# RMSNorm with swish: all transfers issued from SyncE's queue in one written order, with a ring of 100 rows

## The chip, the core and the metric

The kernel runs on one core of a Trainium2 chip. The metric is the time of one execution in device microseconds, as the median of several runs. Beside it stands one execution taken by the hardware profiler, whose span runs from the first to the last instruction of the program. Of the core's engines four are used: VectorE (DVE), ScalarE (ACT), GpSimd (POOL) and SyncE (SP). TensorE does nothing here. Transfers between DRAM and the on-chip memory run on 16 DMA engines, which the queues of SyncE (q1 in the profile) and ScalarE (q10) share.

## The reference

The input x has 16 x 1024 rows of 512 floats. Each row is divided by its root mean square, multiplied by gamma and put through swish:

```python
rms = np.sqrt(np.mean(x ** 2, axis=-1, keepdims=True) + eps)
x_norm = x / rms * gamma
return (x_norm * (1.0 / (1.0 + np.exp(-x_norm)))).astype(np.float32)
```

The 16384 rows of 2 KB are 33.55 MB in and as much out.

## The kernel before, in words

The 16384 rows lie as 128 partitions times 128 rows, so "a row" below means one row of each partition: 128 x 512 floats, 256 KB. The rows are cut into groups of 16, 16, 32, 32, 16 and 16; inside a group each partition holds neighbouring rows of DRAM, so that a piece of n rows is one run of n x 2 KB for each partition.

All rows live in one buffer, `xb`, a ring of 96 rows (line 29); row a sits at place a modulo 96, is loaded there, normalised and swished in place, and stored from there. Rows 96 to 127 reuse places 0 to 31, so they can be loaded only when the first stores have landed.

Compute goes by chunks of four rows (`cn`), 32 chunks, k = 0 to 31, each through four steps:

- `square(k)` on ScalarE: two rows with a sum accumulated along the way (line 181, into `junk`), two rows squared into PSUM (line 188, `sq`). Before it ScalarE waits for the load that holds the chunk (line 178).
- `sums(k)` on VectorE reduces `sq` (line 234), and GpSimd adds eps and takes the power -1/2 (lines 162 and 169).
- `norm(k)` on VectorE multiplies each of the four rows by its factor and gamma (line 245).
- `swish(k)` on ScalarE, one instruction on four rows (line 200).

ScalarE's program is written out as square(k), then swish(k - 2); VectorE's as sums(k), then norm(k - 1). Each engine runs its instructions in the order written.

Transfers are lists of pieces (first row, number of rows). SyncE issues the ten loads (line 125): seven at the start, one after the other, then rows 96 to 127 in three pieces, each after waiting for the stores that empty its places (line 123; `behind` lets load (96,16) also wait for store (16,12)). ScalarE issues the eight stores (line 210) between its own computing: a store stands in ScalarE's program two chunks after its rows are done, and `hold` moves the first three stores to chunk 12, behind a wait for load (64,28) (line 208), and the fourth and later ones to chunk 22 or after, behind a wait for load (112,12). SyncE waits for the remaining stores at the end (line 267).

Two small transfers, a blank one to scratch (line 214) and gamma (line 218), go out on ScalarE's queue at the start. The change leaves them, the compute steps and their order as they are.

Of the kernel before, what the change touches and what calls it, by code (L numbers as in the profile page):

```python
# [9 lines left out]
def kernel(  # L10
# [7 lines left out]
    nc = tc.nc  # L18
# [5 lines left out]
    xf = x.flatten_outer_dims()  # L24
    of = out.flatten_outer_dims()
    R, D = xf.shape

    groups = [16, 16, 32, 32, 16, 16]
    ring = 96
    loads = [(0, 4), (4, 4), (8, 8), (16, 16), (32, 32), (64, 28)]  # L30
    loads += [(92, 4), (96, 16), (112, 12), (124, 4)]
    stores = [(0, 16), (16, 12), (28, 4), (32, 32), (64, 32)]
    stores += [(96, 16), (112, 8), (120, 8)]
    hold = {0: ((64, 28), 12), 3: ((112, 12), 22)}
    behind = {(96, 16): (16, 12)}
    early = 2
    cn = 4
    n_sq = 2
# [9 lines left out]
        assert sum(n for _, n in pieces) == rows_each  # L48

    K = rows_each // cn  # L50
    hold = {t: (loads.index(piece), k) for t, (piece, k) in hold.items()}
    behind = {loads.index(a): stores.index(b) for a, b in behind.items()}
    landings, seen = [], 0
    for k in range(K):
        landings.append([])
# [4 lines left out]
    ends = [-(-(a + n) // cn) for a, n in stores]  # L60
# [20 lines left out]
    ld = [nc.alloc_semaphore(f"ld{t}") for t in range(len(loads))]  # L81
    st = [nc.alloc_semaphore(f"st{t}") for t in range(len(stores))]
# [14 lines left out]
    s_swish = nc.alloc_semaphore("s_swish")  # L97

    def need(ins, sem, value):
        return ins.wait_op(sem, value, "sem-ge")  # L100

    def dram(ap, piece):
        a, n = piece
        g = max(g for g in range(len(groups)) if first[g] <= a)
        r = a - first[g]
        assert r + n <= groups[g], piece
        rows = ap[P * first[g] : P * (first[g] + groups[g])]
        return rows.rearrange("(p n) d -> p n d", n=groups[g])[:, r : r + n, :]

    def buf(piece):  # L110
        a, n = piece
        at = a % ring
        assert at + n <= ring, piece
        return xb[:, at : at + n, :]

    stored_by_sync = set()

    def load(i):
        a, n = loads[i]
        for u, (c, m) in enumerate(stores):  # L120
            over = c + ring < a + n and a < c + m + ring
            if (over or behind.get(i) == u) and u not in stored_by_sync:
                nc.sync.wait_ge(st[u], 16)
                stored_by_sync.add(u)
        return nc.sync.dma_start(  # L125
            out=buf(loads[i]), in_=dram(xf, loads[i])
        ).then_inc(ld[i], 16)

    entry = nc.main_func.blocks[0].instructions
    here = nc.cur_bb.bb.instructions  # L130
# [11 lines left out]
    for t in range(early):  # L142
        ins = load(t).ins
        assert here[-1] is ins or here[-1].name == ins.name
        here.pop()
        at = next(
            i for i, other in enumerate(entry)
            if other.engine == mybir.EngineType.SP
            and isinstance(other, mybir.InstDrain)
        )  # L150
        entry.insert(at, ins)
    for t in range(early, len(loads)):
        load(t)
    nc.sync.wait_ge(s_scratch, 16)

    nc.gpsimd.memset(blank, 0.0).then_inc(s_blank, 1)  # L156
# [3 lines left out]
    for k in range(K):  # L160
        need(
            nc.gpsimd.tensor_scalar(  # L162
                out=aeps[:, k, :], in0=ms[:, k, :], scalar1=eps_f, scalar2=None,
# [6 lines left out]
                out=rstd[:, k, :], in0=aeps[:, k, :], in1=neg_half, op=ALU.pow  # L170
# [4 lines left out]
    def square(k):  # L175
        at = k * cn % ring
        for landing in landings[k]:
            nc.scalar.wait_ge(ld[landing], 16)  # L178
        for j in range(n_sq, cn):
            n = k * (cn - n_sq) + j - n_sq  # L180
            acc = nc.scalar.activation(  # L181
                out=junk[n % 2], in_=xb[:, at + j, :], func=AF.Square,
                scale=inv_d**0.5, accum_out=ms[:, k, j : j + 1],
            )
            if n >= 2:
                need(acc, s_acc, n - 1)
            acc.then_inc(s_acc, 1)
        square = nc.scalar.activation(  # L188
            out=sq[k % 2], in_=xb[:, at : at + n_sq, :],
            func=AF.Square, scale=inv_d**0.5,  # L190
        )
        if k >= 2:
            need(square, s_sum, k - 1)
        square.then_inc(s_sq, 1)

    def swish(k):
        at = k * cn % ring
        rows = xb[:, at : at + cn, :]
        need(
            nc.scalar.activation(out=rows, in_=rows, func=AF.Silu), s_norm, k + 1  # L200
        ).then_inc(s_swish, 1)

    def after(t):
        return max((k for u, (_, k) in hold.items() if u <= t), default=0)

    def store(t):
        if t in hold:
            nc.scalar.wait_ge(ld[hold[t][0]], 16)
        need(
            nc.scalar.dma_start(out=dram(of, stores[t]), in_=buf(stores[t])),  # L210
            s_swish, ends[t],
        ).then_inc(st[t], 16)

    need(nc.scalar.dma_start(out=scratch, in_=blank), s_blank, 1).then_inc(
        s_scratch, 16
    )
# [2 lines left out]
        s_zero, 1,  # L219
    ).then_inc(s_gld, 16)  # L220
    nc.scalar.preload_act_table_set("silu_and_others")  # L221
    stored = 0
    for k in range(K + 3):
        if k < K:
            square(k)
        while stored < len(stores) and max(ends[stored] + 2, after(stored)) <= k:
            store(stored)
            stored += 1
        if 2 <= k < K + 2:
            swish(k - 2)  # L230

    def sums(k):
# [29 lines left out]
        if k >= 1:  # L262
            norm(k - 1)

    for t in range(len(stores)):
        if t not in stored_by_sync:
            nc.sync.wait_ge(st[t], 16)


# [33 lines left out]
```

## Time and profile before

| | before |
|---|---|
| time, median of 3 runs (lowest to highest) | 160.34 us (160.22 to 160.51) |
| span of the profiled execution | 159.3 us (159.28) |
| what lies around the span, median less span | 1.06 us |
| ScalarE busy | 129.7 us, 81% |
| VectorE busy | 124.4 us, 78% |
| GpSimd busy | 65.4 us, 41% |
| bytes moved | 67.17 MB, mean 422 GB/s |
| share of queue q1 (loads), of q10 (stores), of the 16 DMA engines' time | 49.7%, 49.0% |

In the profile's lines an engine's name with a q behind it (SPq, ACTq) is that engine's sequencer, which issues transfers. A line of the timeline has the start and the length in microseconds, the engine, the line of the code, the operation, output and inputs, and in brackets how long the engine had stood idle and what ended that. A piece is named by its first row and number of rows, so load (32,32) is rows 32 to 63. A DMA issue has a time "to landing", from the issue until the semaphore of the last of the 16 DMA engines reports; issue time plus that time is when the piece is in.

### The profile page before, as it was taken

Reading aid. Unit: us, or ns where it says so; the run is one execution under the profiler, and the core shown is the slowest. Engines: PE = TensorE matmul, PEld = TensorE weight load, DVE = VectorE, ACT = ScalarE, POOL = GpSimd, SP = SyncE. Lnnn points to the kernel's source line nnn. Section 1 sums busy time; section 2 is a strip of 40 time slices with the busy share of each in tenths; the row PEclk is TensorE's granted clock in tenths of the full one; section 3 lists DMA queues with packets and bytes.
Section 4 is the critical chain, followed back from the end, with each engine's and each line's share of the span. In section 5 each row is a group of like instructions: output and inputs, shape, how many; then the busy total and the mean of one; then the engine's idle time right before and its main releaser. Section 6 shows DMA issues by size and latency. Waiting matters only on the chain.

```text
span 159.3 us, 503 instructions
## 1 busy us (share of the span) xinstructions
DVE 124.4 (78%) x162; ACT 129.7 (81%) x193; POOL 65.4 (41%) x71
## 2 busy tenths in 40 slices
DVE  0049996999289999599999999999999999992000
ACT  0675979997499995999999999999999999945000
POOL 1035553555145555155555555555555555540000
DMA  7999997998999969999899898969969969999997
GB/s 251 448 467 407 411 593 329 510 444 362 461 432 446 461 280 446 477 399 426 370 397 411 387 469 379 609 280 510 527 263 527 527 263 527 395 395 395 440 420 325
DMA packets 2750, 67.17 MB, mean 422 GB/s; under 512 B 437, under 2 KB 437, under 8 KB 441
## 3 DMA queue, kind: packets, MB, share of 16 engines
q1 hardware_dynamic: 1440, 33.56, 49.7%
q10 hardware_dynamic: 1304, 33.57, 49.0%
q14 instruction: 6, 0.04, 0.1%
HBM read 33.56 MB, written 33.56 MB: 421 GB/s over the span
## 4 chain that ended last, share of the span: by engine, by line
ACT 57%; DMA 25%; DVE 4%; issue 3%; ACTq 1%; SPq 0%
ACT xb L200 25%; DMA xb<-in_x_dram 25%; ACT junk L181 18%; ACT sq L188 14%; DVE xb L245 3%; ACTq L210 1%; DVE ms L234 1%; SPq L125 0%; ACTq L178 0%
## 5 line engine op out<-in xcount | busy, mean ns | idle before, releaser
L245 DVE SCALAR_TENSOR_TENSOR xb<-xb,rstd,gamma_sb 128x512 f32<-128x512 f32 x128 | 87.3, 744 | 0.0
L200 ACT ACTIVATE xb<-xb 128x2048 f32<-128x2048 f32 x32 | 60.9, 1903 | 5.0 <-DVE xb L245 3.4
L234 DVE TENSOR_REDUCE ms<-sq 128x2 f32<-128x1024 f32 x32 | 39.2, 1223 | 19.0 <-ACT sq L188 16.0
L162 POOL TENSOR_SCALAR aeps<-ms 128x4 f32<-128x4 f32 x32 | 20.6, 644 | 71.6 <-DVE ms L234 71.6
L169 POOL TENSOR_TENSOR rstd<-aeps,neg_half 128x4 f32<-128x4 f32 x32 | 44.0, 1376 | 2.7
L181 ACT ACTIVATE junk<-xb 128x512 f32<-128x512 f32 x64 | 37.2, 582 | 6.3 <-DMA xb<-in_x_dram 6.3
L188 ACT ACTIVATE sq<-xb 128x1024 f32<-128x1024 f32 x32 | 32.1, 1005 | 0.0
L181 ACT ACTIVATION_READ_ACCUMULATOR junk<-xb 128x1 f32 x64 | 11.9, 186 | 0.0
L221 ACT ACT_TABLE_LOAD x1 | 1.3, 1283 | 5.4 <-issue 5.4
L258 DVE LOAD_MASK_SELECT gamma_sb<-gamma x1 | 0.0, 14 | 1.1 <-DMA gamma<-in_gamma_dram 1.1
L258 DVE STREAM_SHUFFLE gamma_sb<-gamma 128x512 f32<-128x512 f32 x1 | 0.7, 716 | 0.0
L156 POOL MEMSET blank<- 128x16 f32 x1 | 0.1, 111 | 1.1 <-POOLq L66 1.1
L157 POOL MEMSET gamma<- 128x512 f32 x1 | 0.5, 524 | 0.0
L284 POOL MEMSET const-float32-0.0<- 128x1 f32 x1 | 0.1, 98 | 0.7 <-issue 0.7
L284 POOL MEMSET const-bfloat16-1.0<- 128x1 bf16 x1 | 0.1, 101 | 0.0
L284 POOL MEMSET const-uint8-127<- 128x1 uint8 x1 | 0.1, 101 | 0.0
L158 POOL MEMSET neg_half<- 128x4 f32 x1 | 0.1, 101 | 0.0
L284 POOL MEMSET const-float32-1.0<- 128x1 f32 x1 | 0.1, 99 | 0.0
## 6 DMA issues: line engine op xcount, KB each, us to landing
xb<-in_x_dram SPq DMA_DIRECT2D x2, 4096.0 KB, 16.3
out_dram<-xb ACTq DMA_DIRECT2D x2, 4096.0 KB, 15.3
xb<-in_x_dram SPq DMA_DIRECT2D x1, 7168.0 KB, 55.8
xb<-in_x_dram SPq DMA_DIRECT2D x4, 1024.0 KB, 13.6
out_dram<-xb ACTq DMA_DIRECT2D x2, 2048.0 KB, 13.7
out_dram<-xb ACTq DMA_DIRECT2D x1, 3072.0 KB, 19.6
xb<-in_x_dram SPq DMA_DIRECT2D x1, 3072.0 KB, 19.0
xb<-in_x_dram SPq DMA_DIRECT2D x1, 2048.0 KB, 11.1
```

The source lines that it names most:

```text
L157: nc.gpsimd.memset(gamma4, 0.0).then_inc(s_zero, 1)
L162: nc.gpsimd.tensor_scalar(out=aeps[:, k, :], in0=ms[:, k, :], scalar1=eps_f, scalar2=None, op0=ALU.add,),
L169: nc.gpsimd.tensor_tensor(out=rstd[:, k, :], in0=aeps[:, k, :], in1=neg_half, op=ALU.pow),
L181: acc = nc.scalar.activation(out=junk[n % 2], in_=xb[:, at + j, :], func=AF.Square, scale=inv_d**0.5, accum_out=ms[:, k, j : j + 1],)
L188: square = nc.scalar.activation(out=sq[k % 2], in_=xb[:, at : at + n_sq, :], func=AF.Square, scale=inv_d**0.5,)
L200: nc.scalar.activation(out=rows, in_=rows, func=AF.Silu), s_norm, k + 1
L210: nc.scalar.dma_start(out=dram(of, stores[t]), in_=buf(stores[t])),
L221: nc.scalar.preload_act_table_set("silu_and_others")
L234: nc.vector.tensor_reduce(out=ms[:, k, 0:n_sq], in_=sq[k % 2], op=ALU.add, axis=mybir.AxisListType.X,),
L245: ins = nc.vector.scalar_tensor_tensor(out=row, in0=row, scalar=rstd[:, k, j : j + 1], in1=gamma_sb, op0=ALU.mult, op1=ALU.mult,)
L258: nc.vector.stream_shuffle(gamma_sb, gamma4, [0] * 32), s_gld, 16
L284: nc = _bacc.Bacc("TRN2", target_bir_lowering=False, num_devices=1)
```

## The change

Rows are grouped as 28, 32, 40 and 28, and the ring holds 100 rows. A written list, `order`, has every load, every store, and two kinds of waits: "landed" waits for a load, "stored" for a store. SyncE works through it from the top, and ScalarE issues no load or store of rows any more. As before, the first two loads are placed ahead of the program's start (`early`).

The order is: eight loads (rows 0 to 99); wait for load (60,32); store (0,28) and (28,8); wait for store (0,28); load (100,20) and (120,8) into the places of the first 28 rows; wait for load (100,20); store (36,24), (60,32), (92,8) and (100,28). Each store instruction itself waits until the swishes of its rows are done.

```diff
-    groups = [16, 16, 32, 32, 16, 16]
-    ring = 96
-    loads = [(0, 4), (4, 4), (8, 8), (16, 16), (32, 32), (64, 28)]
-    loads += [(92, 4), (96, 16), (112, 12), (124, 4)]
-    stores = [(0, 16), (16, 12), (28, 4), (32, 32), (64, 32)]
-    stores += [(96, 16), (112, 8), (120, 8)]
-    hold = {0: ((64, 28), 12), 3: ((112, 12), 22)}
-    behind = {(96, 16): (16, 12)}
+    groups = [28, 32, 40, 28]
+    ring = 100
+    loads = [(0, 4), (4, 4), (8, 8), (16, 12), (28, 16), (44, 16), (60, 32), (92, 8)]
+    loads += [(100, 20), (120, 8)]
+    stores = [(0, 28), (28, 8), (36, 24), (60, 32), (92, 8), (100, 28)]
+    order = [("load", a) for a in (0, 4, 8, 16, 28, 44, 60, 92)]
+    order += [("landed", 60), ("store", 0), ("store", 28)]
+    order += [("stored", 0), ("load", 100), ("load", 120)]
+    order += [("landed", 100)] + [("store", a) for a in (36, 60, 92, 100)]
...
+    def store(t):
+        need(
+            nc.sync.dma_start(out=dram(of, stores[t]), in_=buf(stores[t])),
+            s_swish, ends[t],
+        ).then_inc(st[t], 16)
...
-    for t in range(early, len(loads)):
-        load(t)
+    for what, a in order[early:]:
+        if what == "load":
+            load(load_at[a])
+        elif what == "store":
+            store(store_at[a])
+        elif what == "landed":
+            nc.sync.wait_ge(ld[load_at[a]], 16)
+        else:
+            nc.sync.wait_ge(st[store_at[a]], 16)
     nc.sync.wait_ge(s_scratch, 16)
...
-    def store(t):
-        if t in hold:
-            nc.scalar.wait_ge(ld[hold[t][0]], 16)
-        need(
-            nc.scalar.dma_start(out=dram(of, stores[t]), in_=buf(stores[t])),
-            s_swish, ends[t],
-        ).then_inc(st[t], 16)
...
-    stored = 0
-    for k in range(K + 3):
+    for k in range(K + 2):
         if k < K:
             square(k)
-        while stored < len(stores) and max(ends[stored] + 2, after(stored)) <= k:
-            store(stored)
-            stored += 1
-        if 2 <= k < K + 2:
+        if k >= 2:
             swish(k - 2)
```

The rest of the diff is a check of the list while the program is built, and the final waits on SyncE, which now leave out the store that `order` has waited for.

More of the change, by code (lines that the diff above doesn't have):

```diff
@@ L50 @@
     K = rows_each // cn
-    hold = {t: (loads.index(piece), k) for t, (piece, k) in hold.items()}
-    behind = {loads.index(a): stores.index(b) for a, b in behind.items()}
+    load_at = {a: t for t, (a, _) in enumerate(loads)}
+    store_at = {a: t for t, (a, _) in enumerate(stores)}
     landings, seen = [], 0
@@ L114, in buf, with load, check_order @@
         return xb[:, at : at + n, :]
[L116 to L124, printed above, removed]
-        return nc.sync.dma_start(
-            out=buf(loads[i]), in_=dram(xf, loads[i])
-        ).then_inc(ld[i], 16)
+    def load(t):
+        return nc.sync.dma_start(
+            out=buf(loads[t]), in_=dram(xf, loads[t])
+        ).then_inc(ld[t], 16)
+    def store(t):
[3 more added lines that the diff above has]
+        ).then_inc(st[t], 16)
+    def check_order():
+        issued, stored = [], set()
+        for what, a in order:
+            if what == "stored":
+                stored.add(a)
+            if what == "load":
+                n = loads[load_at[a]][1]
+                for c, m in stores:
+                    if c + ring < a + n and a < c + m + ring:
+                        assert c in stored, (a, c)
+            issued.append((what, a))
+        assert [a for what, a in issued if what == "load"] == list(load_at)
+        assert [a for what, a in issued if what == "store"] == list(store_at)
+    check_order()
     entry = nc.main_func.blocks[0].instructions
@@ L151 @@
         entry.insert(at, ins)
-    for t in range(early, len(loads)):
-        load(t)
+    for what, a in order[early:]:
+        if what == "load":
+            load(load_at[a])
[5 more added lines that the diff above has]
+            nc.sync.wait_ge(st[store_at[a]], 16)
     nc.sync.wait_ge(s_scratch, 16)
@@ L201, in swish @@
         ).then_inc(s_swish, 1)
-    def after(t):
-        return max((k for u, (_, k) in hold.items() if u <= t), default=0)
-    def store(t):
-        if t in hold:
-            nc.scalar.wait_ge(ld[hold[t][0]], 16)
-        need(
-            nc.scalar.dma_start(out=dram(of, stores[t]), in_=buf(stores[t])),
-            s_swish, ends[t],
-        ).then_inc(st[t], 16)
     need(nc.scalar.dma_start(out=scratch, in_=blank), s_blank, 1).then_inc(
@@ L263 @@
             norm(k - 1)
-    for t in range(len(stores)):
-        if t not in stored_by_sync:
+    waited = {a for what, a in order if what == "stored"}
+    for t, (a, _) in enumerate(stores):
+        if a not in waited:
             nc.sync.wait_ge(st[t], 16)
```

## The prediction

> **What bounds the kernel now.** I read the page's slices first, then the windows, the DMA issues, the waits, and the chain of waits.
>
> ```profile
> DMA  7999997998999969999899898969969969999997
> GB/s 251 448 467 407 411 593 329 510 444 362 461 432 446 461 280 446 477 399 426 370 397 411 387 469 379 609 280 510 527 263 527 527 263 527 395 395 395 440 420 325
> ...
> q1 hardware_dynamic: 1440, 33.56, 49.7%
> q10 hardware_dynamic: 1304, 33.57, 49.0%
> ...
> HBM read 33.56 MB, written 33.56 MB: 421 GB/s over the span
> ```
>
> Queue q1 (SyncE: the loads) and q10 (ScalarE: the stores) together fill 98.7% of what the 16 DMA engines have. The end is therefore set by the transfers; the bytes stay the same, so a change can only win what is not transfer. The windows (length, busy time of DVE, ACT and POOL, clock, DMA share, GB/s) show where that lies:
>
> ```profile
> 60.00:76.00 16.00, 13.78 (x19) 14.34 (x21) 6.70 (x7) 1.00 1.01 431
> 76.00:84.00 8.00, 7.76 (x11) 8.00 (x13) 4.11 (x5) 1.00 0.98 384
> 84.00:100.00 16.00, 15.52 (x21) 16.00 (x25) 8.22 (x9) 1.00 0.97 419
> 101.00:157.00 56.00, 42.29 (x56) 42.60 (x59) 20.94 (x21) 1.00 0.97 421
> ```
>
> Only 76 to 84 falls behind: 384 against about 425 GB/s is 0.8 us lost, where the loads of rows 96 to 123 start behind a store.
>
> **The price of a row** (128 partitions x 2 KB). Issue time plus the time to landing gives each piece's landing. Load (16,16) landed at 2.28 + 20.5 = 22.8, load (32,32) at 42.1 (the chain's 2.77 + 39.34): 32 rows in 19.3, 0.605 us a row. Stores (64,32), (96,16), (112,8), (120,8) landed at 115.86 + 23.9 = 139.8, 131.83 + 17.7 = 149.5, 139.81 + 14.6 = 154.4 and 146.47 + 12.8 = 159.2: 0.61 us a row, pieces of 8 to 32 rows alike. The first four rows landed at 5.6; the other 252 at 0.605 give 158.0. The kernel lands its last byte at 159.2, so about 1.2 us is to be had and no more.
>
> **ScalarE (ACT) comes second, close behind**:
>
> ```profile
> ACT junk L181 <- DMA xb<-in_x_dram: 6.3, 3, 3.3
> ...
> ACT xb L200 <- issue: 1.7, 1, 1.7
> ```
>
> ```profile
> 22.83 0.60 ACT L181 ACTIVATE junk<-xb 128x512 f32<-128x512 f32 x1 [1.07 <-DMA xb<-in_x_dram]
> ...
> 42.19 0.60 ACT L181 ACTIVATE junk<-xb 128x512 f32<-128x512 f32 x1 [3.28 <-DMA xb<-in_x_dram]
> ...
> 59.49 2.52 ACTq L210 DMA_DIRECT2D out_dram<-xb  x2
> ...
> 62.05 1.91 ACT L200 ACTIVATE xb<-xb 128x2048 f32<-128x2048 f32 x1 [1.66 <-issue]
> ...
> 144.53 1.91 ACT L200 ACTIVATE xb<-xb 128x2048 f32<-128x2048 f32 x1 [0.74 <-DVE xb L245]
> 146.47 0.34 ACTq L210 DMA_DIRECT2D out_dram<-xb  x1
> ```
>
> In a run without stalls a chunk of four rows costs ACT 3.99 us (squares at 63.87 and 135.71, 18 chunks apart). The brackets give three stalls: 1.07 for load (16,16), 3.28 for load (32,32), 1.66 for issuing two stores. The last swish ends at 146.44, only 12.8 us before the end, and an 8-row store of 4.9 us follows an already full queue.
>
> **The change, part by part.**
>
> *Loads in smaller pieces.* Chunk 4 starts when rows 16 to 27 are in, four rows earlier: 22.75 - 4 x 0.605 = 20.3, before ACT's own time (the swish at 19.86 plus the 1.82 to the next square, as from 29.01 to 30.83): 21.68. Chunk 7 is due at 21.68 + 3 x 3.99 = 33.7 and rows 28 to 43 land at 20.3 + 16 x 0.605 = 30.0; chunk 11 at 49.6 against 39.7; chunk 15 at 65.5 against 59.1. No wait is left. The first three loads are the same, so is the wait of 1.97 at 13.1.
>
> *Stores and their waits leave ACT's queue.* The 1.66 us goes; the five later issues cost ACT nothing now (squares stay 3.99 apart across 98.7, 115.9 and 131.8). DVE, the next engine, needs 1.14 + 2.73 = 3.87 us a chunk, so ACT keeps its 3.99. The square of chunk 31 comes at 21.68 + 27 x 3.99 = 129.4 instead of 135.71; the tail behind it (10.73 us to the last swish's end) stays. **The last swish ends at 140.2**, 6.2 us earlier: 1.07 + 3.28 + 1.66, and 0.2 of restart.
>
> *All on SyncE, one direction at a time.* Eight issues of some 0.4 us leave ACT for SyncE. Behind each wait stand all later transfers, but each leaves 8 rows queued, 8 x 0.605 = 4.8 us. Issue to first packet was 0.86 us for a store (59.11, first q10 packets in the window from 59.96) and 0.9 to 1.0 for a load (79.2 and 80.1). Even with the up to 2 us between a DMA's first and last engine the cover holds. Without it each costs about 1 us, as between 76 and 84 where only four rows stood behind.
>
> On landings, which are those of the slowest engine: load (92,4), the first 96 rows, is in at 3.83 + 57.7 = 61.5 today; 100 rows then at 63.9. Store (0,28) lands at 80.8, (28,8) at 85.6, load (100,20) at 97.7, (120,8) at 102.6, stores (36,24) at 117.1, (60,32) at 136.5, (92,8) at 141.3. Their swishes are early (7 chunks at about 41.6, 9 at 49.7, 15 at 73.6, 23 at 105.6, 25 at 113.5: the second square after a chunk's own, plus 4 us), so no store but the last waits on ACT. Chunk 25 is squared at 21.68 + 21 x 3.99 = 105.5, 8 us after its rows land. The last store, **28 rows where it was 8**, would land at 141.3 + 28 x 0.605 = 158.2 if it were queued in time.
>
> *It is not.* It needs all 32 swishes: 140.2, plus 0.06 to reach SyncE, plus 0.9 to the first packet: 141.2. A landing follows its last packet by about 0.45 us, so the slowest engine is empty at 140.8 and most of them, about 0.8 earlier, at 140.0. From 141.2, 28 rows take 16.95 to 158.1, some 0.1 for spread between engines and 0.45 for the landing: 158.7. The end is now ACT's chain and one long store.
>
> How an empty queue takes a store is not in this trace; bounds: from below the 0.9 + 0.45 us above (158.6); from above the very first load, 5.6 us from issue to landing of which four rows are 2.4, so 3.1 us fixed: 140.26 + 3.1 + 16.95 = 160.3. I take the store row: same direction, warm, and its packets took no longer than later ones.
>
> The Trainium skill (DMA: Bandwidth & Descriptors, Anatomy of one DMA) puts about 2.0 us of fixed cost on a transfer, mostly the receipt of the last write, measured on GpSimd's path. By it the last store would land at 140.26 + 2.0 + 16.95 = 159.2, an estimate by which the span stays what it is; the nearest row, 0.9 + 0.45, gives 158.6, and no lone store in this trace tests it.
>
> *Smaller edits.* Two transfers fewer, other row strides in DRAM (28 and 40 rows where there were 16 and 32): nothing, since 0.605 held for strides of 16 and 32 rows; if the strides were not harmless, every percent on the 155 us of transfer would be 1.5 us less 1.1, for the last store waits for ACT until the transfers are 0.4 to 1.2 us late. The final waits on SyncE end as now, 0.05 us after the last landing.
>
> *Sum.* Span 158.75 against 159.28, 0.53 less. The median of the runs, 160.34, lies 1.06 above the profiled span; I keep that: 159.8 us.
>
> **Rivals.**
> 1. *ACT's tail does not bind*: the swishes end before about 139.6 or the start is quicker, and the transfers run through: landing 158.2, time 159.3. Against: every term of 140.2 is a row of the trace, and it needs 0.6 us less.
> 2. *The long store's start costs more* than a queued one: with 1.35 to 3.1 us fixed the span is 158.8 to 160.3, the time 159.9 to 161.4. For it: the cold load at 0, whose 3.1 us fixed are a row of this trace. Against: that was the first access of the run. The page on DMA named above stands on this side, with 160.3 as its estimate.
> 3. *Turning round on one queue costs, slower than before.* Three times (store behind load at 63, load behind store at 85, store behind load at 102) both directions now share one ring. At 80.1 the first load packets after stores were long: in 80.1 to 82.4 q1's 30 packets filled 127.1% of 16 engines, 127.1% x 2.3 x 16 / 30 = 1.56 us each, where 32 KB at 425/16 GB/s take 1.23. Two packets so stretched on each engine are 0.7 us; three turns put 2.0 on the 158.2: span 160.25, time 161.3. It passes today's span once the turns cost more than 1.1 us together. Against: at 100.3 stores followed loads without a gap, and the loads of 80.1 met an idle queue.
> 4. *The change does not do what it says*: SyncE's order lets a transfer through late, for instance when the queue refuses an eighth load until one has landed. That would delay only rows 92 to 99, due 30 us later: no change of time from it.
>
> **How the numbers follow.** Forecast (159.5 to 160.1) 0.55; rival 1 0.08; rival 2 beyond 160.1 0.20; rival 3 0.13; rest 0.04. About 0.2% (0.3 us) is what a measurement can tell from no change: faster means under 160.02. Faster: 0.48 of the forecast and 0.08: 0.56. Same: 0.07 of the forecast, 0.11 of rival 2, 0.02: 0.20. Slower: 0.09, 0.13, 0.02: 0.24. The range runs from rival 1 less its spread, 159.1, to the upper bounds of rivals 2 and 3, 161.4.
>
> **What would show it.** ACT should wait for loads only at 13.1 and never on issue; the last swish should end near 140.2, the last store be issued by SyncE at 140.3 with its first packet near 141.2 and land 18.4 us after issue. A gap in the DMA slices before 140 on any engine speaks for rival 3; over 19 us from issue to landing, for rival 2. The forecast is wrong if the last swish is off by more than 0.4 us, or if the queue still holds work at 141.2.

## The result and the profile after

The changed kernel takes 162.59 us (median of 4 runs, 162.38 to 162.66), beside 160.43 us for the kernel before in the same session. The ratio is 1.014, with a 95% interval of 1.0127 to 1.0154. It is slower by 2.2 us, where 159.8 us was forecast.

ScalarE did what was forecast. Its waits in the profile after, and its last instructions in the timeline, are these (columns as before: start, length, engine, line, operation, idle time before it and what ended that):

```profile
ACT xb L222 <- DVE xb L252: 3.2, 3, 2.1
ACT junk L203 <- DMA xb<-in_x_dram: 1.5, 1, 1.5
```

```profile
13.13 0.60 ACT L203 ACTIVATE junk<-xb 128x512 f32<-128x512 f32 x1 [1.52 <-DMA xb<-in_x_dram]
...
138.14 1.91 ACT L222 ACTIVATE xb<-xb 128x2048 f32<-128x2048 f32 x1 [0.74 <-DVE xb L252]
140.08 0.33 SPq L124 DMA_DIRECT2D out_dram<-xb  x1
```

One wait for a load is left, that at 13.1. The 1.7 us on issuing are gone. The last swish ends at 140.05 instead of 146.44, and SyncE issues the last store at 140.08. So 6.4 us were won on ScalarE, and the kernel still ends 2.2 us later. The transfers tell where:

```profile
GB/s 250 436 449 420 469 430 398 471 430 414 519 471 308 519 321 398 457 457 455 361 457 363 426 436 388 442 438 450 499 361 503 422 390 394 489 426 369 455 455 43
DMA packets 2461, 67.17 MB, mean 416 GB/s; under 512 B 404, under 2 KB 404, under 8 KB 408
## 3 DMA queue, kind: packets, MB, share of 16 engines
q1 hardware_dynamic: 2304, 67.11, 97.6%
```

The last slice moves 43 GB/s where it moved 325. Of the 16 DMA engines, few are still at work then. The DMA view of the window from 158.5 to 161.2 us says how many:

```profile
q1 hardware_dynamic: 9, 0.17, 14.8%
```

The 0.17 MB are three packets of 57 KB, the last of three engines; no other engine starts a packet of data in this window. The landing records of the trace (one for each DMA engine and transfer) agree: the last store has landed on the median engine at 158.41 us, on the last three at 161.09, 161.20 and 161.45. In the kernel before the median engine came at 158.92 and the last at 159.23. So the middle of the engines became faster by 0.5 us, and the end is set by three engines that are 3 us behind. The landings in order (median engine / last engine, us; the pieces of the two kernels differ, so those next to the same turn stand in one row):

| | before | after |
|---|---|---|
| last load before the first turn | 60.44 / 61.51 | 63.31 / 66.35 |
| last store before the second turn | 80.00 / 81.53 | 85.23 / 87.86 |
| first load after it | 91.14 / 91.31 | 97.94 / 99.97 |
| last load before the third turn | 100.93 / 101.06 | 102.84 / 105.87 |
| last store | 158.92 / 159.23 | 158.41 / 161.45 |

A "turn" below is where the queue changes direction: from loads to stores at 62 us (first), from stores to loads at 84 us (second), back to stores at 102 us (third). The table says where the three fell behind. Load (60,32) landed at 58.16 (median) and 59.14 (last), 1.0 apart, as at the start. Load (92,8), the next on the queue, landed at 63.31 and 66.35, 3.0 apart; two engines are that late there, the third joins them with the loads after the second turn. The distance shrinks to 2.0 at load (100,20), since the other engines lost time at that turn, and is back at 3.0 at load (120,8), before the third turn. SyncE issued its transfers at these times:

```profile
0.00 4.82 SPq L118 DMA_DIRECT2D xb<-in_x_dram  x8
59.22 0.82 SPq L124 DMA_DIRECT2D out_dram<-xb  x2
83.05 0.82 SPq L118 DMA_DIRECT2D xb<-in_x_dram  x2
100.03 40.38 SPq L124 DMA_DIRECT2D out_dram<-xb  x4
```

The first store had thus been queued behind load (92,8) at 59.22. The packets in the window from 61.0 to 62.4 stand beside those of 58.2 to 60.2 (number of packets, MB, share of 16 engines' time):

```profile
DMA packets 54, 0.85 MB, mean 426 GB/s; under 512 B 2, under 2 KB 2, under 8 KB 2
...
q1 hardware_dynamic: 54, 0.85, 99.7%
```

```profile
DMA packets 30, 0.49 MB, mean 351 GB/s; under 512 B 0, under 2 KB 0, under 8 KB 0
...
q1 hardware_dynamic: 30, 0.49, 116.6%
```

In the first window the 52 packets of 16 KB take 99.7% x 2.0 x 16 / 52 = 0.61 us each. In the second, 30 of them take 116.6% x 1.4 x 16 / 30 = 0.87 us each. Here the last loads before the first stores slow down, and the store's own packets have not yet begun: the first starts at 62.9.

### The profile page after: what moved, and what is told of

It reads as the page before. It is cut to its first block, busy times and chain, and to the rows that moved or that the text cites. A ratio compares the mean times of both kernels' runs of the same rounds, so it can differ in the third digit from the quotient of the medians.

```text
span 161.5 us, 500 instructions
## 1 busy us (share of the span) xinstructions
DVE 124.4 (77%) x162; ACT 129.4 (80%) x193; POOL 65.4 (41%) x71
## 4 chain that ended last, share of the span: by engine, by line
ACT 66%; issue 8%; DVE 6%; DMA 5%; POOL 0%; POOLq 0%
ACT xb L222 27%; ACT junk L203 22%; ACT sq L210 16%; DMA gamma<-in_gamma_dram 5%; DVE xb L252 5%; DVE ms L241 1%; DVE gamma_sb L265 0%; POOL gamma L179 0%; POOL blank L178 0%; POOLq L67 0%
```

## The experiments

"Cover" is the rows that are still queued in the old direction when the other direction is issued; the changed kernel has 8 at each turn. "Lag" is the landing on the last engine less that on the median engine. "Excess" is the time of slow packets over the usual time of their size, summed and divided by 16. Both come from the packet and landing records of the trace, and so from the one execution of each version that was profiled. Ratios are against the kernel before in the same session.

Three theories went into the first four runs: the one queue (A), the new pieces (B), and the cover, which lets no turn bring the engines level (C).

### Stores on ScalarE's queue again

```diff
+    on_act = {0: (13, 60), 28: (13, None), 36: (24, 100), 60: (25, None), 92: (27, None), 100: (34, None)}
...
-            nc.sync.dma_start(out=dram(of, stores[t]), in_=buf(stores[t])),
+            queue.dma_start(out=dram(of, stores[t]), in_=buf(stores[t])),
...
```

> The changed kernel with the same pieces, ring and waits, but with every store issued by ScalarE (queue q10) again, at the place in ScalarE's program where its turn comes. Theory A (one queue: where loads and stores stand one behind the other on one queue, the packets next to the turn get slow, on a few DMA engines by 2 to 3 us, and nothing waits for those engines until the end): the lag between the median and the last of the 16 engines at the landing of load (92,8) falls from 3.0 us to about 1.1, that of the last store to under 0.7, and the time is 159.6 to 160.2. Theory B (the pieces: runs of 28 and 40 rows in DRAM and transfers of 7 MB): it stays at 162 to 163. Theory C (8 rows of cover: no turn lets the engines come level again, so whatever lag there is adds up): lags near 3 us in spite of two queues, and 161.5 to 162.5.

Measured: 161.23 us (160.52 to 162.59 over 8 runs), ratio 1.0063 (1.0033 to 1.0092). Better than one queue, and still slower than before. The load packets slow down as well; in the window from 61.0 to 62.4 us:

```profile
q1 hardware_dynamic: 24, 0.39, 100.7%
```

That is 100.7% x 1.4 x 16 / 24 = 0.94 us for 16 KB. Load (92,8) lands on its last engine at 69.88 us (median 63.34), since on the late engines the stores of the other queue now go between its packets. Theory A does not explain this: with two queues the loss is there.

### The kernel before, with its stores on SyncE's queue

```diff
+    order = [("load", a) for a in (0, 4, 8, 16, 32, 64, 92)]
+    order += [("landed", 64)] + [("store", a) for a in (0, 16, 28)]
+    order += [("stored", 0), ("stored", 16), ("load", 96), ("load", 112)]
+    order += [("stored", 28), ("load", 124)]
+    order += [("landed", 112)] + [("store", a) for a in (32, 64, 96, 112, 120)]
...
```

> The kernel before with its own groups, ring and pieces, with one edit: all its stores go out on SyncE's queue, in the same order and behind the same waits for landings. Theory A: slow packets at each turn, the last engine 2 to 3 us behind the median at the end; 161 to 163 us. Theory B: nothing lost, and ScalarE is rid of 1.7 us of issuing; 159.9 to 160.4. Theory C: as before, 160.0 to 160.6, since its turn at 79 us waits for the last engine with only 4 rows of cover and brings the engines level.

Measured: 160.22 us, ratio 1.0004 (0.9992 to 1.0017). One queue by itself costs nothing, and theory A falls. That ScalarE got rid of its issues brought nothing either: the last store is issued at 144.72 instead of 146.47 and waits in a full queue, 14.7 us to its landing instead of 12.8.

The Trainium skill (DMA: Bandwidth & Descriptors, Issuing engines are not separate DMA queues) says that transfers issued by different engines share the same 16 DMA engines, so that several issuers save issuing time only. The ratio of 1.0004 agrees for these pieces. With the new pieces issuing time is not all: two queues had a ratio of 1.0063 where one had 1.014.

### The first two stores on ScalarE's queue, the rest on SyncE's

```diff
+    on_act = {0: (13, 60), 28: (13, None)}
...
```

> The changed kernel, with only the first two stores, (0,28) and (28,8), issued by ScalarE; all else stays on SyncE's queue. Only the third turn (stores behind load (120,8)) is then on one queue. Theory A: the last engine at the landing of load (92,8) is at most 1.2 us behind the median; slow packets remain at 101 to 104 us alone; the end between the two others, 160 to 161.5 us. Theories B and C: no change, 162 to 163.

Measured: 161.90 us, ratio 1.0114 (1.0096 to 1.0131). The lag at the landing of load (92,8) is 6.9 us (63.10 and 70.03), again because stores overtake it, and that of store (0,28) 2.4 us (2.8 with one queue). Slow load packets stand at 61 to 62 us and, few (six), at 101 to 104. Theory A had a lag of 1.2 at the first turn.

### Each turn after everything has landed

```diff
-    order += [("landed", 60), ("store", 0), ("store", 28)]
-    order += [("stored", 0), ("load", 100), ("load", 120)]
-    order += [("landed", 100)] + [("store", a) for a in (36, 60, 92, 100)]
+    order += [("landed", 92), ("store", 0), ("store", 28)]
+    order += [("stored", 0), ("stored", 28), ("load", 100), ("load", 120)]
+    order += [("landed", 120)] + [("store", a) for a in (36, 60, 92, 100)]
```

> The changed kernel on its one queue, but each turn waits until all that was queued has landed: store (0,28) for load (92,8), load (100,20) for store (28,8), store (36,24) for load (120,8). No cover: each turn costs some 1.5 to 2 us of idle DMA engines. Theory A: with nothing queued behind them the load packets before a turn keep their 0.61 us, the lag at the landing of load (92,8) is 1.0 us, and every turn brings the engines level: 161.5 to 163.5 us, the last engine under 0.5 us behind the median at the end. Theory B: 3 us lag in spite of it, 164 to 167. Theory C expects level engines as well, and so tells itself from A here only by the packets before the turn.

Measured: 166.16 us, ratio 1.0374 (1.0358 to 1.0389). With nothing queued behind them the loads before the first turn keep their pace: no 16 KB packet is over 0.62 us. After each turn the engines are level, at the end within 0.1 us. But the idle time is more than expected: 3.3 us of the engines' time at the first turn, 1.7 at the second, 1.6 at the third. At the first, one engine's landing came 1.1 us after all others, right after an instruction fetch (8 KB on another queue), and the turn waited for it. Of theory A's claims the packets before the turn hold, but two queues showed the same slowness; so what is left is the cover, called theory D from here on.

This kernel also shows transfers that meet idle engines. Store (0,28), issued at 65.07 us, and load (100,20), issued at 88.37 us:

```profile
out_dram<-xb SPq DMA_DIRECT2D x1, 7168.0 KB, 18.4
```

```profile
xb<-in_x_dram SPq DMA_DIRECT2D x1, 5120.0 KB, 14.6
```

Less 28 x 0.605 = 16.95 and 20 x 0.605 = 12.1, the fixed part is 1.4 us for the store and 2.5 us for the load.

### Which part of the cover: time, packet size, or row stride

The next four runs set the cover against the size of the packets (16 KB) and the strides in DRAM (80 KB in the group of 40 rows).

```diff
-    loads = [(0, 4), (4, 4), (8, 8), (16, 12), (28, 16), (44, 16), (60, 32), (92, 8)]
+    loads = [(0, 4), (4, 4), (8, 8), (16, 12), (28, 16), (44, 16), (60, 32), (92, 4), (96, 4)]
-    order += [("landed", 60), ("store", 0), ("store", 28)]
+    order += [("landed", 92), ("store", 0), ("store", 28)]
```

> The changed kernel with the last 8 rows of the first loads as two pieces, (92,4) and (96,4), and the first stores waiting for (92,4) instead of (60,32): 4 rows of load stand before the first store at the turn, not 8; the other two turns keep their 8. What the first four runs left: theory A, one queue, fell (two queues lose as well, old pieces on one queue lose nothing). Theory D (cover): a store that reaches the DMA engines while each still has 3 or 4 load packets to do lets the late engines fall behind, since their loads are slow while the others already store. Then the lag at the landing of the last of the first loads is 1.0 to 1.5 us here (3.0 in the changed kernel), few load packets are slow at 60 to 63 us, and the time is 160.2 to 161.5. Theory P (packets of 16 KB): lag under 1.5 as well, since the packets are 8 KB here; the next run tells. Theory S (row strides of 80 KB in DRAM in the group of 40): lag stays near 3, 162 to 163.

Measured: 161.79 us, ratio 1.0095 (1.0080 to 1.0110). The lag at the landing of load (96,4) is 1.4 us, and no load packet is slow at 60 to 63 us. The ratio fell from 1.014 to 1.0095, about 0.7 us and less than expected, because the third turn now lost more: the excess over the usual packet time there is 0.95 us for each engine, 0.34 in the changed kernel.

The same split, with the stores still waiting for load (60,32):

> The same split into (92,4) and (96,4), but the stores still wait for (60,32), so that 8 rows of load stand before the first store as in the changed kernel; only the packets are 8 KB instead of 16. Theory D: no gain, lag 2 to 3 us or more, 162 to 163. Theory P: lag 1.0 to 1.5 us, 160.2 to 161.5. Theory S: lag near 3.

Measured: 162.20 us, ratio 1.0113 (1.0085 to 1.0142), lag 3.5 us. Small packets are no remedy.

```diff
-    groups = [28, 32, 40, 28]
+    groups = [28, 32, 32, 8, 28]
```

> The changed kernel with its group of 40 rows cut into groups of 32 and 8, so that load (92,8) and its store run through one closed stretch of DRAM (partitions 16 KB apart) and (60,32) too (64 KB apart). Theory S: lag 1.0 to 1.5 us at the landing of load (92,8), 160.2 to 161.5. Theories D and P: no change, lag near 3, 162 to 163.

Measured: 162.53 us, ratio 1.0128 (1.0108 to 1.0148), slow packets as before. The lag of 2.1 us lies between the two expectations, but time and packets show no part of the strides in it. The next version takes the rest from theory B: it keeps the runs of 28 and 40 rows and the transfers of 7 MB.

```diff
...
+    loads += [(100, 20), (120, 4), (124, 4)]
+    stores = [(0, 28), (28, 4), (32, 4), (36, 24), (60, 32), (92, 8), (100, 28)]
+    order = [("load", a) for a in (0, 4, 8, 16, 28, 44, 60, 92, 96)]
+    order += [("landed", 92)] + [("store", a) for a in (0, 28, 32)]
+    order += [("stored", 0), ("stored", 28)] + [("load", a) for a in (100, 120, 124)]
+    order += [("landed", 120)] + [("store", a) for a in (36, 60, 92, 100)]
```

> The changed kernel with 4 rows of cover at all three turns: pieces (92,4), (96,4), stores (28,4), (32,4), loads (120,4), (124,4); each turn waits for the transfer before the last one queued. Theory D: lags of 1.0 to 1.8 us at the first turn, the second turn costs idle time and slow first packets as in the kernel before (1.2 us) and brings the engines level (lag under 0.6 after it), the end is 159.5 to 160.8. Theories P and S as above; S: 162 or more.

Measured: 160.55 us (160.25 to 160.89 over 10 runs), ratio 1.0019 (1.0007 to 1.0030). With half the cover, all but 0.3 us of the loss is gone. In the window from 61.0 to 62.4 us the loads, now in packets of 8 KB, keep their pace:

```profile
DMA packets 72, 0.53 MB, mean 380 GB/s; under 512 B 7, under 2 KB 7, under 8 KB 7
...
q1 hardware_dynamic: 72, 0.53, 91.5%
```

65 packets take 91.5% x 1.4 x 16 / 65 = 0.315 us each, 0.31 elsewhere. The landings are 98.52 and 98.87 (median and last) after the second turn and 159.06 and 159.36 at the end. One expectation missed: the lag at the first turn is 2.1 us, not 1.0 to 1.8. It is one engine alone (the next is 1.1 us behind the median), and an instruction fetch stands at 63.5 us, as with drained turns.

### Is it the turn, or the store's arrival on the queue?

```diff
-    order += [("landed", 60), ("store", 0), ("store", 28)]
+    order += [("landed", 44), ("store", 0), ("store", 28)]
```

> The changed kernel with the first stores waiting for load (44,16) instead of (60,32): store (0,28) is issued as soon as its swishes are done, near 42 us, and stands on the queue behind 20 us of loads instead of 3. If what hurts is that each engine has a store behind its last loads (theory D1, the turn itself), the slow load packets stay at 60 to 63 us, the lag is about 3 us and the time 162 to 163. If it is the arrival of the store's descriptors (D2), packets are slow from 42 us on and the lag at 60 us is already over 2 us; 162.5 to 165.

Measured: 162.75 us, ratio 1.0173 (1.0157 to 1.0189). The store is issued at 41.64 us. Packets are slow from 59.7 to 63 us and not before, and the lag at the landing of load (60,32) is the usual 1.15 us. It is the turn: the last few load packets of each engine, wherever the store has been waiting. A little more is lost than in the changed kernel (1.014): the excess at the first turn is 1.1 us, 0.6 there.

### Cover of 6 and of 3 rows at the second turn

```diff
-    stores = [(0, 28), (28, 4), (32, 4), (36, 24), (60, 32), (92, 8), (100, 28)]
+    stores = [(0, 28), (28, 2), (30, 6), (36, 24), (60, 32), (92, 8), (100, 28)]
```

> The version with 4 rows of cover at all turns (160.55 us), with 6 rows at the second: stores (28,2) and (30,6). Theory D: less idle time than the 0.8 us there, but the late engines still have stores to do when the loads come, so the lag after the turn is 1 to 2 us instead of 0.3: 160.3 to 161.5. If cover were only good (as the prediction had it): 159.7 to 160.0.

Measured: 161.19 us, ratio 1.0076 (1.0058 to 1.0093); idle time at the turn falls from 0.81 to 0.01 us, and the lag after it is 1.7 us, at the end 1.1.

> The same with 3 rows at the second turn: stores (28,5) and (33,3). Theory D: the engines come level, and 0.6 us more are idle: 160.8 to 161.4. The lag after the turn under 0.5 us.

Measured: 160.95 us, ratio 1.0057 (1.0041 to 1.0073); idle time 1.05 us, the engines level (lag 0.4 us). Both are slower than 4 rows (1.0019), as expected.

### Turn by turn

Each of three runs gives 8 rows of cover to one turn alone, 4 to the two others.

> Cover of 4, 4 and 8 rows at the first, second and third turn. Theory D with lateness as its cause (an engine loses at a turn because it is late there and the others already move the other way): the second turn brings the engines level, so 8 rows at the third cost little: 160.4 to 161.0, lag at the end under 1 us. Theory D by turn (every turn with 8 rows of cover loses 1 us or more, late or not): 161.2 to 162, lag at the end over 1.2 us.

Measured: 161.60 us, ratio 1.0079 (1.0061 to 1.0096). The engines come to the third turn level, and all of them lose: load (120,8) lands at 104.56 and 105.03 (median and last). The lag at the end is 0.5 us, not over 1.2, but the time is that of the second form: an engine need not be late to lose at this turn. The loads in the window from 101.0 to 102.4 us, here and in the version with 4 rows at all turns:

```profile
DMA packets 35, 0.57 MB, mean 410 GB/s; under 512 B 0, under 2 KB 0, under 8 KB 0
...
q1 hardware_dynamic: 35, 0.57, 136.6%
```

```profile
DMA packets 70, 0.57 MB, mean 410 GB/s; under 512 B 0, under 2 KB 0, under 8 KB 0
...
q1 hardware_dynamic: 70, 0.57, 96.7%
```

The packets that start in this window, 0.57 MB in both, take 136.6% of the engines' time in it (the last ones end behind it), and 96.7% where no store is queued that early.

> Cover of 4, 8 and 4 rows. The engines come to the second turn with the lag of the first, 1.8 us, and 8 rows leave them so: lag over 1.5 us after it and at the end, 161.0 to 161.9 by both forms of theory D, since the last store ends on the slowest engine. If cover at the second turn were harmless: 160.0 to 160.6.

Measured: 160.69 us (160.07 to 161.39 over 10 runs), ratio 1.0030 (1.0009 to 1.0051). This expectation missed: by the median, 8 rows of cover at the second turn cost hardly anything. The stores before that turn are slow here (16 KB packets at 83.4 to 84.6 us, an excess of 0.79 us), but no engine idles, and in the profile the lag after the turn is 0.7 us, not 1.5. With 4 rows the same turn costs 0.81 us of idle time and 0.55 of slow packets. The profiled execution is one of the shortest of the ten (160.17 us), and why 6 rows cost more (1.0076) than 8 is open. What cover does at the second turn is therefore not settled.

> Cover of 8, 4 and 4 rows. The first turn loses as in the changed kernel (lag near 3 us); the second waits for the slowest engine and brings the engines level at its time, so the lag is gone (under 1 us) but not the time: 161.3 to 162.2. If the median engine set the end: 160.5.

Measured: 161.62 us, ratio 1.0089 (1.0060 to 1.0119). The first turn loses (lag 3.3 us), the second waits for the slowest engine, with 1.86 us of the engines idle, and brings them level (lag 0.4 us) at its time.

The turns add up. Over the version with 4 rows everywhere (1.0019), 8 rows cost 1.0089 - 1.0019 = 0.0070 at the first turn (1.1 us), 0.0011 at the second (0.2 us) and 0.0060 at the third (1.0 us). Each difference is good to about 0.5 us, so that of the second turn is no more than noise. The sum, 0.0141, put on 1.0019 gives 1.016; the changed kernel has 1.014.

### Without the computing

```diff
-    for k in range(K + 2):
+    for k in range(0):
```

and the same for the loops of GpSimd and VectorE; the stores do not wait for swishes, but for the landings of the loads whose rows they send.

> The changed kernel with all its transfers in the same order and with the same cover, but without the computing: no square, sum, power, norm or swish, stores send out what the loads brought, and wait for landings alone. Theory D (what is lost at the turns is among the transfers themselves): the lag at the landing of load (92,8) is still 2 to 3 us, at the end 2 us or more, and the time 161 to 162.6. Theory E (the computing engines' access to the on-chip buffer is what slows the packets next to a turn): lag about 1.1, end at 158.2 plus 1.1, so 159.0 to 159.6.

Measured: 160.83 us, ratio 1.0067 (1.0039 to 1.0095). The first turn is as with computing: lag 2.0 us, and the load packets of 61.0 to 62.4 us take 120.9% x 1.4 x 16 / 30 = 0.90 us each. That contradicts theory E. The second and third turns lost nothing here, though, and the time fell short of the expected 161. At the third turn SyncE waited for the late engines and issued at 99.35, so it remained open whether the computing has a part there. The last two runs test that:

> Transfers only, without any computing, cover of 4 rows at all three turns. The base for the next run; 159.8 to 160.6 us, as with computing (160.55) or up to 0.7 less, since it is the transfers that set the end there.

> The same with 8 rows of load before the stores of the third turn. If the loss is among the transfers alone: slow load packets at 101 to 104 us, about 0.9 us on each engine, and 0.8 to 1.2 us more than the run before. If the computing's use of the on-chip buffer has a part in it: less than half of that, under 0.5 us more.

Measured: 160.39 us (159.92 to 161.95 over 10 runs), ratio 1.0032 (0.9998 to 1.0065), and 161.04 us (160.82 to 162.89 over 8 runs), ratio 1.0066 (1.0030 to 1.0103). In the two profiles the excess of the packets at the third turn is 0.03 and 0.75 us for each engine, the spans are 159.2 and 160.2 us. The medians lie 0.65 us apart, between the two expectations, and the intervals overlap. Both versions scatter: five of the ten runs of the first lie between 159.92 and 160.13 us and four above 161.3, six of the eight of the second between 160.82 and 161.13 and two above 162.5. The lower ones are some 0.9 us apart, as the first expectation had it, and the two profiles, which are of such runs, 1.0 us. The slow packets come without any computing.

Why the third turn of the first run without computing lost nothing can be read from all the versions whose stores go out on SyncE's queue at that turn. What counts there is how long before the median landing of the last load the first store is issued. Where that is 2.1 us or less, at the first turn or the third, the excess before the turn is under 0.1 us; at 2.5 to 3.6 us it is 0 to 0.5, at 3.9 to 5.3 us 0.6 to 0.95, and 1.1 where the store stood on the queue for 22 us. (Slow packets lengthen this time too, by as much as the excess.) At the third turn the store waits for load (100,20) on the last engine, so late engines shorten the time for all others: 2.7 us in the first run without computing, 2.8 in the changed kernel, with an excess of 0.01 and 0.34, but 4.7 to 5.3 us where the engines come more nearly level (0.75 to 0.95). This is an ordering of the profiles, not a test of its own.

## Why the prediction was wrong, point by point

**The price of a row** was right: on the median engine store (60,32) landed 19.30 us after store (36,24), 0.603 us a row for 0.605. **The sum of rows** was not. The prediction had the slowest engine run through to 158.2 and most engines some 0.8 us earlier; the median engine landed at 158.41, about 1.0 us later than that. That it comes so near the forecast's 158.7 is chance: the forecast had the engines empty before the last store, and on fourteen of the 16 it followed store (92,8) without a gap.

**ScalarE** was right: the waits left, the last swish at 140.05 for 140.2, the store's issue at 140.08 for 140.26.

**The step that failed** is "but each leaves 8 rows queued ... the cover holds. Without it each costs about 1 us". It took the cover as free and its absence as the cost. In the sum the turns therefore stand at nothing. The runs show the reverse for two of three turns: 8 rows of loads with a store queued behind them cost 1.1 us at the first turn and 1.0 us at the third, 4 rows cost next to nothing there. In the changed kernel this put load (92,8) at 66.35 us where 63.9 was forecast, and the last landing at 161.45 where it was 158.7. The only turn that the trace of before showed as costly, the one at 80 us, is of the other direction. The two turns from loads to stores looked free in that trace, where only 4 rows stood before each.

**"The slowest engine is empty at 140.8"** failed with it. Store (92,8), issued at 113.48, landed at 144.56 on the last engine, so the late engines still had work when the last store was issued, and ScalarE's earlier end bought nothing there. On the three late engines the first packets of the last store began at 143.9 to 144.2, where 141.2 was forecast. It took 21.4 us from issue to landing, for the 18.4 of the forecast (the lines of the two stores):

```profile
out_dram<-xb SPq DMA_DIRECT2D x1, 2048.0 KB, 31.1
```

```profile
out_dram<-xb SPq DMA_DIRECT2D x1, 7168.0 KB, 21.4
```

**Rival 2, the start of a lone store,** did not come up in the changed kernel, although the 21.4 us pass the 19 that the prediction gave as its sign: the store stood in a queue that still held work. The version with drained turns measured it: 1.4 us, as the row of before had it (0.9 + 0.45). The Trainium skill's 2.0 us (DMA: Bandwidth & Descriptors, Anatomy of one DMA), given for GpSimd's path, is too high for a store on this queue and too low for the load that follows stores, with 2.5 us; of these some 0.6 are its slow first packets.

**Rival 3, turning round,** named the right mechanism with too small a chance, 0.13, and 161.3 us for the 162.6 measured. Its sign, a gap in the DMA slices before 140, did not show: no slice before 140 is below 7 tenths, since slow packets leave no gap. Its argument was partly wrong. The one queue is not what costs (1.0004). The price was taken from the first load packets after stores, where the loss is in the last load packets before stores. And it spread its loss evenly, where the first turn puts two engines 1 to 2 us further back than the rest. Rival 4 did not come up: all eight loads were issued within 4.82 us.

Theory C, that a turn with little cover brings the engines level, holds as a part of it. In the kernel before, the second turn, with its short cover, waits for the last engine, and so clears the lag of the first (1.5 us at store (28,4), 0.2 us at load (96,16)). In the changed kernel the engines work on through all three turns, and the last store ends on whichever engine is latest.

Why the last load packets slow down when a store stands behind them is not settled. Neither a single queue, nor packets of 16 KB, nor the row stride, nor the computing is needed for it.

## What to carry to other kernels

These runs are of one kernel; elsewhere the advice has to be tried. Where loads and stores share the DMA engines, do not queue a store early behind a long tail of loads. Try the cover small, so that the store reaches the engines as the loads run out, and look at the packets next to the turn. Before work is moved off an engine that is not the bound, check what the last transfer waits for: 6 us won on ScalarE were worth nothing here while the transfers set the end. And read the landings of all 16 DMA engines, not the mean: a transfer lands with the slowest, and a mean of 416 GB/s hides three engines that are 3 us late.

## What the runs showed of the hardware that was not expected

- In the changed kernel load packets of 16 KB take 0.61 us, and 0.87 us (window mean) shortly before a store that is queued behind them; singly up to 1.55 us. The first load packets after stores are slow in most versions, 0.4 to 0.8 us for each engine in all, even after idle time (0.62 with drained turns). Less was lost at that turn where ScalarE had issued the stores before it (0.08 and 0.15) and in the first run without computing (0.02); why is open.
- The DMA engines do not stay level by themselves: in the kernel before, a lag of 1.0 us from the first packets of the program stays for 58 us of loads and more, until the second turn, with its little cover, clears it.
- None of the versions beats the kernel before. The best of the new order, 4 rows at all turns, has a ratio of 1.0019 (1.0007 to 1.0030): it still loses 0.8 us of idle engines and 0.55 us of slow packets at the second turn, as the kernel before does (0.57 and 0.66).
